# Pairs of weight blocks by seven products: the last sum of a chain by an accumulating transfer, the stream's steps spread over all 28 steps of a pair

## The chip, the cores and the metric

The kernel runs on one core of a Trainium2 chip. The metric is the device time of one execution in microseconds (us). Five engines work beside each other, each through its own instruction list in order: PE (TensorE: matrix products, with its weight loads shown as PEld), DVE (VectorE), ACT (ScalarE), POOL (GpSimd) and SP (SyncE, which here only issues DMA transfers). The transfers run on 16 DMA engines that all queues share. Products go to PSUM, everything else lies in SBUF.

## The reference

Two layers over 256 tokens of width 2048, in float32, then a last norm:

```python
x = x + even_layer(x, ...)     # norm, one wide projection, a gated linear recurrence, dilated attention, projection back
x = x + odd_layer(x, ...)      # the layer in which the change lies
return rms_norm(x, final_norm)

def odd_layer(x, norm, w_in, ...):
    h = rms_norm(x, norm)
    z = h @ w_in               # 2048 -> 512, 512, 1024, 16, 1024, 1024, 1024, 1024
    q, k, v, a_lr, gc, u, vd, gd = jnp.split(z, ...)
    ...                        # chunked linear attention from q, k, v; spatial gating from u, vd; gates gc, gd
    return jnp.concatenate([yc, yd], axis=-1) @ w_out
```

The change touches only how `h @ w_in` is computed for q with k, for the two halves of vd, and for the two halves of u.

## The kernel before, in words

**A weight tile.** Weights come from HBM in tiles of 128 x 1024 float32 (512 KB: two of the 16 k-tiles, 512 columns each). Products run in a rounded format, so every tile is split first (`parts`, L135): ACT casts it to `whi` (L138), DVE subtracts to get `wlo` (its line shows as L73, that of the helper). There are four `whi` and four `wlo` tiles, so a tile can be cast as soon as PE is done with the fourth tile before it. Each product is three matmuls of 512 columns (high by high, high by low, low by high).

**Two kinds of work.** A plain block (`token_steps`) multiplies each weight tile with both token blocks: 12 matmuls a tile (L146 to L148). A *pair* takes two column blocks of 512 at once, splits tokens and rows of the weights into halves, and needs seven products of half size instead of eight (a scheme of the Strassen kind): 7 x 4 = 28 steps of one tile and 6 matmuls each (L251 to L253). There are three pairs, one after the other: q with k (units 6 and 10 of `w_in1`), vd (14, 18) and u (30, 34). Four plain blocks, the gates, are the *stream* between the pairs' steps: 32 stream steps, of which the pairs take 10, 8 and 10, and the last four come after the third pair.

**The steps of a pair** (numbered 0 to 27 here, four to a product):

- 0 to 3: product into `m12` from the tiles `x0` (block a, upper rows); after a step has split its tile, POOL issues an accumulating transfer (L245) that adds block b's upper rows to the tile in place. Before each step SP is handed the fetch of a tile of `y0` (block b, lower rows).
- 4 to 7: `m3` from `y0`; then block b's upper rows are added to `y0` in the same way.
- 8 to 11: `m56` from the new `x0`; then block b's lower rows are added to `x0`.
- 12 to 15: `m7` from the new `y0`.
- 16 to 19: `m56` again, from the new `x0`.
- 20 to 23: `m12` again, from fresh tiles `z0` (block a, lower rows), fetched by SP.
- 24 to 27: `m4` from `x0` with block a's lower rows added.

In the kernel before the last of these sums is one DVE instruction a tile, `x0 + z0` (L299), and the steps of the last two products alternate: `z0[0]`, `z0[1]`, `z0[2]`, `m4` 0, `z0[3]`, `m4` 1, 2, 3. The adds are held in program order among them. When the seven products are there, DVE joins them (L279 to L283, L301). During the steps of `z0` the first tiles of the next pair are fetched too (`onward`, into the buffers that `y0` has left).

**Buffers and queues.** Tiles rest in three rings: `raw` with three buffers (stream tiles and `z0`), `rx` and `ry` with four each (`x0` and `y0`, whose roles swap from pair to pair). All fetches go through SP's one queue, whose instructions wait in order for their buffer to come free. The accumulating transfers go through POOL's queue.

**The order.** `weave` (L217) decides where stream steps stand: after each step of the pair it lets the stream go on while `done * 17 < taken * count`, so all stream steps of a pair stand among its first 17 steps (for a count of 10: after steps 0, 1, 3, 5, 6, 8, 10, 11, 13 and 15). Small tasks (the linear attention, the gates, transposes) are interleaved by `tick`, which counts steps.

Of the kernel before, what the change touches and what calls it, by code (L numbers as in the profile page):

```python
# [13 lines left out]
ALU = mybir.AluOpType  # L14
# [37 lines left out]
def trunk(ctx, tc, x, xt, lead, w_in0, w_out0, w_va, w_in1, w_out1, w_gate, small, dist, cst, w_alpha, w_s,  # L52
          r_balpha, r_vnorm, r_fnorm, out):
    nc = tc.nc
# [29 lines left out]
    def mid_tile(shape, name, dtype=F32):  # L84
        return mid.tile(shape, dtype, name=name, tag="mid")
# [13 lines left out]
    def tick(n):  # L99
        for task in list(tasks):  # L100
            task[1] -= n
            if task[1] <= 0:
                wait = next(task[0], None)
                if wait is None:
                    tasks.remove(task)
                else:
                    task[1] = wait
# [11 lines left out]
    def raw_tile(shape, tag=None):  # L119
        if tag is None:  # L120
            tag = "raw"
            if not paired[0]:
                turns.append(turns.pop(0))
                tag = turns[-1]
        return rawp.tile(shape, F32, name=tag, tag=tag, bufs=rings[tag])
# [9 lines left out]
    def parts(raw, n=1024):  # L135
        hi = hip.tile([P, n], F32R, name="whi", tag="whi")
        lo = lop.tile([P, n], F32R, name="wlo", tag="wlo")
        nc.scalar.copy(hi, raw)  # L138
        sub(lo, raw, hi)
        return hi, lo  # L140
# [68 lines left out]
    def piece_of(w, u, i):  # L209
        return w[u + i // 2][:, i % 2 * 1024:i % 2 * 1024 + 1024]  # L210

    def fetch(w, u, i, tag):
        raw = raw_tile([P, 1024], tag)
        nc.sync.dma_start(out=raw, in_=piece_of(w, u, i))
        return raw

    def weave(steps, stream, count):  # L217

        done = taken = 0
        while True:  # L220
            try:
                next(steps)
            except StopIteration as end:
                return end.value
            taken += 1
            while done < count and done * 17 < taken * count:
                stream.step()
                done += 1

    def pair(w, ua, ub, act, forms, x0, tag, after=None):  # L230

        f3, f5, f6, f7 = forms

        def step(ps, a, i, raw, first, u=None):
            tile_, k0, b = a
            hi, lo = parts(raw)
            if u is not None:
                nc.gpsimd.dma_start(out=raw, in_=piece_of(w, u, i), accum_op=ALU.add)  # L245
            for kk in range(2):
                j = 2 * i + kk
                wh, wl = hi[:, kk * 512:(kk + 1) * 512], lo[:, kk * 512:(kk + 1) * 512]
                xh = tile_[:, k0 + j, b * P:(b + 1) * P]
                xl = tile_[:, k0 + j, T + b * P:T + (b + 1) * P]  # L250
                nc.tensor.matmul(ps, xh, wh, start=(first and j == 0), stop=False, skip_group_check=not first)  # L251
                nc.tensor.matmul(ps, xh, wl, start=False, stop=False, skip_group_check=not first)  # L252
                nc.tensor.matmul(ps, xl, wh, start=False, stop=(j == 7), skip_group_check=not first)  # L253
                tick(1)

        def run(ps, a, raws, first, u=None):
            for i, raw in enumerate(raws):
                step(ps, a, i, raw, first, u)
                yield

        def bank():
            return psm.tile([P, 512], F32, name="ps", tag="ps")

        m12, m3, m56, m7 = bank(), bank(), bank(), bank()
        y0 = []
        for i, raw in enumerate(x0):
            y0.append(fetch(w, ub + 2, i, tag))
            step(m12, (act, 0, 0), i, raw, True, ub)
            yield
        s1 = mid_tile([P, 512], "s1")  # L270
        nc.scalar.copy(s1, m12)
        yield from run(m3, f3, y0, True, ub)
        yield from run(m56, f5, x0, True, ub + 2)
        s5 = mid_tile([P, 512], "s5")
        nc.scalar.copy(s5, m56)
        yield from run(m7, f7, y0, True)
        yield from run(m56, f6, x0, False)
        t = mid_tile([P, 512], "t")
        nc.vector.tensor_tensor(out=t, in0=m56, in1=s1, op=ALU.subtract)  # L279
        c22 = s1  # L280
        nc.vector.tensor_tensor(out=c22, in0=m7, in1=t, op=ALU.add)
        nc.vector.tensor_tensor(out=t, in0=m3, in1=t, op=ALU.add)
        nc.vector.tensor_tensor(out=s5, in0=s5, in1=c22, op=ALU.subtract)  # L283
        m4 = bank()
        onward = []
        z0 = []
        for i in range(6):
            if i < 4:
                z0.append(fetch(w, ua + 2, i, "raw"))
                step(m12, (act, 8, 0), i, z0[i], False)  # L290
                yield
                if after is not None:
                    onward.append(fetch(w, after, i, tag))
            if i > 1:
                step(m4, (act, 8, 1), i - 2, x0[i - 2], True)
                yield
            if 0 < i < 5:

                tc.keep_in_program_order(nc.vector.tensor_tensor(out=x0[i - 1], in0=z0[i - 1], in1=x0[i - 1],  # L299
                                                                 op=ALU.add))  # L300
        nc.vector.tensor_tensor(out=s5, in0=m4, in1=s5, op=ALU.add)  # L301
        return [m12, s5], [t, c22], onward

# [499 lines left out]
    paired[0] = True  # L803
    x0 = [fetch(w_in1, 6, i, "rx") for i in range(4)]
    ps, ps_k, x0 = weave(pair(w_in1, 6, 10, act2, forms2, x0, "ry", 14), stream, 10)
    drain()
    eb, enb, ebl = decays
# [81 lines left out]
    vf = []  # L889
    mv = tiny.tile([P, 8, 2], F32, name="mv", tag="mv", bufs=1)  # L890
    *vd, x0 = weave(pair(w_in1, 14, 18, act2, forms2, x0, "rx", 30), stream, 8)
    for c, ps in enumerate(vd):
        t = big_tile([P, 2, 512], f"vf{c}")
# [53 lines left out]
    def mix(c, t):  # L947
        yield 2
        for b in range(2):
# [7 lines left out]
            yield 2  # L957

    *ud, _ = weave(pair(w_in1, 30, 34, act2, forms2, x0, "ry"), stream, 10)
    paired[0] = False  # L960
    for c, ps in enumerate(ud):
# [52 lines left out]
    for s in range(4):  # L1014
        raw = raw_tile([P, 4, 256])
# [118 lines left out]
```

## Time and profile before

| | |
|---|---|
| median of 3 runs | 883.27 us (882.65 to 884.69) |
| the profiled execution | 882.66 us, its span 881.0 us |
| PE, PEld | 857.9 us busy (97%), 718.6 us (82%) |
| DVE, ACT, POOL | 610.0 us (69%), 526.3 us (60%), 42.9 us (5%) |
| SP's DMA queue q1 | 152.65 MB, 50.8% of the 16 engines' span |
| POOL's DMA queue q0 | 22.06 MB, 12.6% |

The span runs from the first instruction to the last. Busy time is that of instructions which compute. Matmuls overlap, so the duration of one (389 ns for 512 columns) is longer than the distance from one to the next. A "DMA share" is the time that packets took, over the 16 engines and the stretch. The three pairs run from about 537 us to 767 us.

### The profile page before, as it was taken

To read this page: it belongs to the slowest core of one execution; us is meant where nothing else is said; L and a number is where in the kernel's file an instruction comes from. 1 tells how busy PE (TensorE), PEld (TensorE's weight loads), DVE (VectorE), ACT (ScalarE), POOL (GpSimd) and SP (SyncE) were. 2 spreads that over 40 slices of the span, in tenths; PEclk is the share of its full clock that TensorE was granted. 3 is DMA by queue.
4 is the path that set the end of the run, shared out by engine and by line. 5 is a ranking of instruction groups with operands and counts; after the bars stand their busy time and mean duration, and the time that the engine had idled before them with its cause. 6 is when DMAs were issued, how large, how long until landed. Compare 5 with 4: busy or idle time off the path is not lost.

```text
span 881.0 us, 11887 instructions
## 1 busy us (share of the span) xinstructions
PE 857.9 (97%) x4408; PEld 718.6 (82%) x4408; DVE 610.0 (69%) x867; ACT 526.3 (60%) x764; POOL 42.9 (5%) x60
## 2 busy tenths in 40 slices
PE   8999999999999999999999999998999899899996
PEld 7888888888888888888888988885768578688886
DVE  7676557677576586666555996679748976995652
ACT  7755556666766766554444776565476766654532
POOL 1100000000000000010000002201210121000000
PEclk9999999999999999999999999999999999999999
DMA  9896555555455455565544658967965899665502
GB/s 342 335 366 213 185 194 164 170 169 177 160 177 170 144 172 178 190 208 194 184 135 154 219 184 209 252 225 211 250 144 176 245 254 322 202 220 189 190 2 96
DMA packets 50266, 175.53 MB, mean 199 GB/s; under 512 B 5648, under 2 KB 6160, under 8 KB 49952
## 3 DMA queue, kind: packets, MB, share of 16 engines
q1 hardware_dynamic: 43920, 152.65, 50.8%
q0 software_dynamic: 6144, 22.06, 12.6%
q8 instruction: 34, 0.56, 0.2%
q14 instruction: 24, 0.20, 0.1%
q10 hardware_dynamic: 144, 0.07, 0.0%
HBM read 172.66 MB, written 2.10 MB: 198 GB/s over the span
## 4 chain that ended last, share of the span: by engine, by line
PE 91%; DVE 6%; ACT 1%; issue 1%; DMA 0%; ACTq 0%
PE pc L315 20%; PE ps L147 15%; PE ps L148 15%; PE ps L146 15%; PE pc L314 10%; PE ps L251 3%; PE ps L252 3%; PE ps L253 3%; DVE wlo L73 3%; ACT whi L138 1%; DVE rx L299 1%; PE pc L317 1%; PE sc L500 1%; PE gp L584 1%; PE gp L583 1%
## 5 line engine op out<-in xcount | busy, mean ns | idle before, releaser
L315 PE MATMUL pc<-act,whi 128*128 128x512 f32 x768 | 269.8, 395 | 0.0
L314 PE MATMUL pc<-act,wlo 128*128 128x256 f32 x720 | 208.5, 290 | 0.0
L73 DVE TENSOR_TENSOR wlo<-rx,whi 128x1024 fp32r<-128x1024 f32 (+2 forms) x118 | 141.4, 1199 | 74.9 <-ACT whi L138 73.3
L138 ACT CAST whi<-rx 128x1024 fp32r<-128x1024 f32 (+1 forms) x115 | 119.9, 1044 | 100.3 <-PE ps L148 59.1
L73 DVE TENSOR_TENSOR wlo<-ry,whi 128x1024 fp32r<-128x1024 f32 (+2 forms) x110 | 131.6, 1198 | 67.9 <-ACT whi L138 66.7
L315 PEld LDWEIGHTS pc<-act,whi 128*128 128x128 f32 x768 | 142.6, 188 | 29.4
L138 ACT CAST whi<-ry 128x1024 fp32r<-128x1024 f32 (+1 forms) x108 | 112.2, 1041 | 90.4 <-PE ps L148 53.2
L73 DVE TENSOR_TENSOR wlo<-raw,whi 128x1024 fp32r<-128x1024 f32 (+2 forms) x100 | 119.0, 1190 | 47.7 <-ACT whi L138 45.7
L138 ACT CAST whi<-raw 128x1024 fp32r<-128x1024 f32 (+1 forms) x97 | 100.9, 1040 | 68.0 <-PE ps L148 25.6
L314 PEld LDWEIGHTS pc<-act,wlo 128*128 128x128 f32 x720 | 135.9, 189 | 2.4 <-DVE wlo L73 0.8
L146 PE MATMUL ps<-whi,act 128*128 128x512 f32 (+2 forms) x352 | 131.8, 377 | 1.4 <-DVE la_s L473 1.1
L147 PE MATMUL ps<-wlo,act 128*128 128x512 f32 (+2 forms) x352 | 131.0, 372 | 1.3 <-DVE wlo L73 1.2
L148 PE MATMUL ps<-whi,act 128*128 128x512 f32 (+2 forms) x352 | 130.7, 371 | 0.0
L146 PE MATMUL ps<-whi,yt 128*128 128x512 f32 (+1 forms) x256 | 97.3, 380 | 0.0
L148 PE MATMUL ps<-whi,yt 128*128 128x512 f32 (+1 forms) x256 | 96.4, 376 | 0.0
L147 PE MATMUL ps<-wlo,yt 128*128 128x512 f32 (+1 forms) x256 | 96.2, 376 | 0.0
L146 PEld LDWEIGHTS ps<-whi,act 128*128 128x128 f32 x352 | 66.1, 188 | 15.0 <-issue 2.2
L147 PEld LDWEIGHTS ps<-wlo,act 128*128 128x128 f32 x352 | 66.3, 188 | 13.5 <-DVE wlo L73 2.6
L148 PEld LDWEIGHTS ps<-whi,act 128*128 128x128 f32 x352 | 66.2, 188 | 11.4
L148 PEld LDWEIGHTS ps<-whi,yt 128*128 128x128 f32 x256 | 48.2, 188 | 8.9
L147 PEld LDWEIGHTS ps<-wlo,yt 128*128 128x128 f32 x256 | 48.2, 188 | 8.5
L146 PEld LDWEIGHTS ps<-whi,yt 128*128 128x128 f32 x256 | 48.2, 188 | 8.3
(289 smaller groups left out, 1040.1 us busy)
## 6 DMA issues: line engine op xcount, KB each, us to landing
raw<-in_w_in SPq DMA_DIRECT2D x77, 512.0 KB, 5.2
ry<-in_w_in SPq DMA_DIRECT2D x64, 512.0 KB, 4.7
rx<-in_w_in SPq DMA_DIRECT2D x63, 512.0 KB, 4.6
rx<-in_w_out SPq DMA_DIRECT2D x24, 512.0 KB, 4.3
ry<-in_w_out SPq DMA_DIRECT2D x23, 512.0 KB, 4.0
rx<-in_w_in POOLq DMA_DIRECT2D x20, 512.0 KB, 9.9
raw<-in_w_out SPq DMA_DIRECT2D x17, 512.0 KB, 4.5
ry<-in_w_in POOLq DMA_DIRECT2D x16, 512.0 KB, 8.6
```

Of the source, the lines that this page charges most:

```text
L73: nc.vector.tensor_tensor(out=o, in0=a, in1=hi.bitcast(F32), op=ALU.subtract)
L138: nc.scalar.copy(hi, raw)
L146: nc.tensor.matmul(ps[b], xh, wh, start=first, stop=False)
L147: nc.tensor.matmul(ps[b], xh, wl, start=False, stop=False)
L148: nc.tensor.matmul(ps[b], xl, wh, start=False, stop=last)
L251: nc.tensor.matmul(ps, xh, wh, start=(first and j == 0), stop=False, skip_group_check=not first)
L252: nc.tensor.matmul(ps, xh, wl, start=False, stop=False, skip_group_check=not first)
L253: nc.tensor.matmul(ps, xl, wh, start=False, stop=(j == 7), skip_group_check=not first)
L299: tc.keep_in_program_order(nc.vector.tensor_tensor(out=x0[i - 1], in0=z0[i - 1], in1=x0[i - 1], op=ALU.add))
L314: nc.tensor.matmul(ps[c][:, 1, :], wl, act[:, k, 0:T], start=False, stop=False)
L315: nc.tensor.matmul(ps[c], wh, act[:, k, :], start=(k == 0), stop=(k == KT - 1))
L317: nc.tensor.matmul(ps[c][:, 1, :], wl, act[:, k, 0:T], start=False, stop=False)
```

## The change

The weave spreads a pair's stream steps over all 28 steps: `done * 28 < taken * count` (for a count of 10: after steps 0, 2, 5, 8, 11, 14, 16, 19, 22 and 25; for 8: after 0, 3, 7, 10, 14, 17, 21 and 24). The second run of `m56` now issues an accumulating transfer of block a's lower rows into `x0` after each split, four more for a pair. The DVE adds are gone, the `z0` tiles are no longer kept after their split, and the last two products run one after the other.

```diff
@@ weave
-            while done < count and done * 17 < taken * count:
+            while done * 28 < taken * count:
                 stream.step()
                 done += 1
@@ pair
-        yield from run(m56, f6, x0, False)
+        yield from run(m56, f6, x0, False, ua + 2)
@@
-        z0 = []
-        for i in range(6):
-            if i < 4:
-                z0.append(fetch(w, ua + 2, i, "raw"))
-                step(m12, (act, 8, 0), i, z0[i], False)
-                yield
-                if after is not None:
-                    onward.append(fetch(w, after, i, tag))
-            if i > 1:
-                step(m4, (act, 8, 1), i - 2, x0[i - 2], True)
-                yield
-            if 0 < i < 5:
-                tc.keep_in_program_order(nc.vector.tensor_tensor(out=x0[i - 1], in0=z0[i - 1], in1=x0[i - 1],
-                                                                 op=ALU.add))
+        for i in range(4):
+            step(m12, (act, 8, 0), i, fetch(w, ua + 2, i, "raw"), False)
+            yield
+            if after is not None:
+                onward.append(fetch(w, after, i, tag))
+        yield from run(m4, (act, 8, 1), x0, True)
```

## Rows read from the trace of the kernel before

**Rows 1.** The page's first part: busy us, share of the span, instructions.

```profile
PE 857.9 (97%) x4408; PEld 718.6 (82%) x4408; DVE 610.0 (69%) x867; ACT 526.3 (60%) x764; POOL 42.9 (5%) x60
```

**Rows 2.** Windows: for each pair steps 0 to 15, then 16 to 27.

```profile
core 0: us, PE busy (x) PEld busy (x) DVE busy (x) ACT busy (x) POOL busy (x), PEclk, DMA share, GB/s
537.40:586.40 49.00, 49.00 (x218) 40.56 (x217) 32.50 (x27) 31.29 (x33) 9.42 (x11) 1.00 1.01 265
586.40:609.30 22.90, 18.89 (x76) 13.13 (x75) 21.20 (x23) 12.01 (x13) 0.00 (x0) 1.00 0.47 151
609.30:671.50 62.20, 62.08 (x295) 45.52 (x294) 41.86 (x52) 38.12 (x57) 10.28 (x12) 1.00 0.87 216
671.50:693.80 22.30, 17.94 (x72) 12.83 (x71) 20.48 (x23) 14.57 (x16) 0.00 (x0) 1.00 0.46 156
693.80:745.60 51.80, 50.63 (x224) 41.60 (x223) 41.74 (x56) 33.52 (x36) 11.40 (x14) 1.00 1.02 269
745.60:767.00 21.40, 18.45 (x74) 13.04 (x72) 19.13 (x21) 13.54 (x15) 0.00 (x0) 1.00 0.63 217
```

**Rows 3.** Waits in 586.4 to 609.3: total us, times, longest us.

```profile
ACT whi L138 <- DVE rx L299: 6.1, 4, 3.0
...
ACT whi L138 <- DMA raw<-in_w_in: 3.0, 1, 3.0
PE ps L251 <- ACT whi L138: 2.8, 4, 1.3
```

**Rows 4.** Groups on DVE, 537 to 771: count, busy us, mean ns.

```profile
L73 DVE TENSOR_TENSOR wlo<-rx,whi 128x1024 fp32r<-128x1024 f32 x40 | 48.7, 1220 | 22.9 <-ACT whi L138 21.9
...
L299 DVE TENSOR_TENSOR rx<-raw,rx 128x1024 f32<-128x1024 f32 x8 | 9.7, 1216 | 0.0
L299 DVE TENSOR_TENSOR ry<-raw,ry 128x1024 f32<-128x1024 f32 x4 | 4.9, 1218 | 0.0
```

**Rows 5.** Timeline of PE, an undisturbed step: start us, duration us.

```profile
538.10 0.39 PE L251 MATMUL ps<-whi,act 128*128 128x512 f32 x1
538.32 0.39 PE L252 MATMUL ps<-wlo,act 128*128 128x512 f32 x1
538.55 0.39 PE L253 MATMUL ps<-whi,act 128*128 128x512 f32 x1
```

**Rows 6.** DMA in 543.9 to 581.4: packets, MB, share; issues with us to landing.

```profile
q0 software_dynamic: 1439, 5.24, 73.3%
q1 hardware_dynamic: 1178, 4.30, 30.8%
...
rx<-in_w_in POOLq DMA_DIRECT2D x5, 512.0 KB, 10.0
```

**Rows 7.** Timeline of POOL: issues of the accumulating transfers at steps 1, 11.

```profile
537.66 0.86 POOL L245 DMA_DIRECT2D rx<-in_w_in  x1 [6.12 <-DVE wlo L73]
...
570.94 0.86 POOL L245 DMA_DIRECT2D rx<-in_w_in  x1 [1.93 <-issue]
...
731.93 0.85 POOL L245 DMA_DIRECT2D rx<-in_w_in  x1 [2.62 <-issue]
```

**Rows 8.** Tile `raw` in 537 to 586, 586 to 609, 700 to 745.

```profile
DMA to landing us min/median/max: 5.2/7.9/9.3
...
DMA to landing us min/median/max: 4.0/4.5/5.4
...
DMA to landing us min/median/max: 6.6/8.2/11.7
```

**Rows 9.** Tile `raw` in 537 to 771: cast durations ns min/median/max.

```profile
L138 ACT CAST whi<-raw x40: 1037/1055/1067, 538.2 to 769.0; 128x1024 fp32r<-128x1024 f32 x40
```

**Rows 10.** Timeline of SP: first pair, fetches of `z0[2]`, `z0[3]`.

```profile
581.59 0.33 SPq L214 DMA_DIRECT2D raw<-in_w_in  x1
592.81 0.33 SPq L214 DMA_DIRECT2D raw<-in_w_in  x1
```

**Rows 11.** Timeline of ACT, third pair: cast of `z0[2]`, with its wait.

```profile
751.45 1.05 ACT L138 CAST whi<-raw 128x1024 fp32r<-128x1024 f32 x1 [1.89 <-DMA raw<-in_w_in]
```

## The prediction

> **What bounds the kernel now.** I read the page's busy times first, then windows over the three pairs, then waits, timelines and DMA queues inside them. PE is the bound: 97% of the span, the next engine 69% [rows 1]. So the change can give no more than the time in which PE stands still inside the pairs, and it can take that back by new stops. The windows cut each pair where the stream's steps end [rows 2]. In steps 0 to 15, with all the stream steps between, PE is busy without a gap in the first two pairs, and the 16 DMA engines are full: shares of 1.01, 0.87 and 1.02. In steps 16 to 27 it is the other way round: PE idles 22.9 - 18.9 = 4.0, 22.3 - 17.9 = 4.4 and 21.4 - 18.4 = 3.0 us, 11.3 us together, DVE is busy 21.2 of 22.9 us, and the DMA share falls to 0.47, 0.46 and 0.63. The granted clock is 1.00 in all six.
>
> The waits of the first such tail name the stop: PE's first matmul of a step waits for ACT's cast, and the cast waited 6.1 us for the DVE adds of L299 (four of them) and once 3.0 us for a `raw` transfer [rows 3]. That transfer is `z0[3]`: its fetch is issued at 592.81, 11 us after that of `z0[2]` at 581.59, because the three `raw` buffers are held until the first add is done [rows 10].
>
> So DVE and the ring stop the tails, and the transfers fill the first parts. The change moves work from the first kind of limit to the second.
>
> **What goes.** Twelve adds of 1.22 us (8 and 4) [rows 4] are 14.6 us of DVE. PE's matmuls follow each other every 0.227 us (538.10, 538.32, 538.55) [rows 5]: a pair step of 6 is 1.365 us, a stream step of 12 is 2.73 us. One split costs DVE 1.22 us, so a tail without stream steps asks 16 splits' worth of DVE (12 splits, 4 adds: 19.5 us, and the joining of the products besides) for 12 x 1.365 = 16.4 us of PE. After the change the same 12 pair steps have 4 stream steps among them (3 in the second pair): 16 splits, still 19.5 us, but 16.4 + 10.9 = 27.3 us of PE. DVE is then no limit there. What PE gets back is at least the 11.3 us of idle. At most it is the tails' whole excess over the matmul pace, 22.9 + 22.3 + 21.4 - 3 x 16.4 = 17.4 us, which counts the small tasks' matmuls as if they were free. I take 13.5, nearer to the idle, since those tasks stay.
>
> **What it adds on POOL and the DMA engines.** Four accumulating transfers a pair, 12 in all. POOL's part is 12 x 0.86 us [rows 7], beside an engine busy 5%: nothing, unless the ring behind it is full; POOL already waits by "issue" before step 11's, and nothing but these transfers stands behind it. On the DMA engines the window 543.9 to 581.4 gives the price [rows 6]. q0 holds 73.3% of 37.5 us for 5.24 MB, ten tiles, so 2.75 us a tile; q1 holds 30.8% for 8.2 tiles, 1.41 us a tile. An accumulated tile costs twice a plain one, and the sum for the new ones is 4 x 2.75 = 11.0 us a pair. The `z0` fetches stay. The pairs' DMA time is now 49.5 + 10.8 = 60.3, 54.1 + 10.3 = 64.4 and 52.8 + 13.5 = 66.3 us [rows 2]; it becomes 71.3, 75.4 and 77.3, against PE busy times of 67.9, 80.0 and 69.1. In the first pair and the third the transfers ask as much time as the pair has; some of it is prefetch for what follows (in the third `w_out` tiles) and can be late.
>
> The Trainium skill, DMA: Bandwidth & Descriptors (Anatomy of one DMA), prices a transfer from GpSimd at about 2.0 us fixed, mostly completion, plus bytes / 436e3. By it a 512 KB tile moves in an estimated 1.2 us whatever it does on the way, the 12 would cost 14.4 us instead of 33, and the first rival below is what would come. The rows' 2.75 us speaks against it.
>
> **Are the new sums in time?** From step 16 to step 24 lie 8 x 1.365 + 3 x 2.73 = 19.1 us. An accumulating transfer needs 0.9 to issue and 10.0 to land [rows 6, 7], the cast before the matmul 1.05 [rows 9] and about 0.25 to hand over: 12.2. They are in time with 7 us to spare, so I price them at nothing; the cover is gone if the queue is 7 us behind. The tighter ones are those of steps 8 to 11. The last is issued at 570.94, 33.5 us into the pair, and lands some 10 us later, at 43.5. Step 19 needs it 1.3 us before its start. Before, ten stream steps stand ahead of step 19, after it seven, so it starts 8.2 us sooner, at 19 x 1.365 + 7 x 2.73 = 45.0, and needs its tile at 43.7. The eight us of spare are spent. Fewer stream fetches ahead (three, 4.2 us) give some back. In the third pair the last issue is at 731.93, 38.1 us in. I take 0 and keep 2 us a pair for the range.
>
> **The fetches of `z0`: the new wait.** Steps 19 to 25 now use seven `raw` tiles (stream, `z0[0]`, `z0[1]`, `z0[2]`, stream, `z0[3]`, stream) where a ring of three holds them. `z0[2]` gets the buffer of the stream tile after step 19. That one can be cast when PE is done with the stream step after 16 (four `whi` tiles). From there: cast and subtraction 2.6, issue 0.3, landing L, cast and hand-over 1.3, so 4.2 + L. PE meanwhile works 5 pair steps and one stream step, 9.6 us. The stop is L - 5.4. The stream tile after step 25 hangs on `z0[2]` in the same way: 2.7 + L against 8.2 us, again L - 5.5. Behind the waiting fetch SP holds the `onward` fetches and the next stream tile; the next pair's tiles wait with them, needed only at its first steps.
>
> All depends on L. In the tail of the first pair, where no accumulation runs, it is 4.5 us; in the first part 7.9 (5.2 to 9.3), in the third pair 8.2 and up to 11.7 [rows 8], and there `z0[2]` already kept ACT waiting 1.9 us, at 751.45 [rows 11]. After the change the accumulations run through the tail, and four fetches for what follows stand in the same queue. I take L = 9.0 for `z0[2]` in pairs one and three (between the medians and the longest) and 6.2 for the last stream tile, when the accumulations have nearly landed: 3.6 + 0.7 = 4.3 us each. In the second pair, whose small tasks stretch it and whose DMA share is lower, I take L = 7.0: 1.6 us. Ends: L = 4.5 costs nothing; L = 11.7 and 8 cost 6.3 + 2.5 = 8.8 in two pairs and some 4 in the other, 21.6 us.
>
> **The sum.** 13.5 back, 4.3 + 1.6 + 4.3 = 10.2 us given up again: 3.3 us net. The profiled execution took 882.66 us (1.66 more than its span) and becomes 879.4; the median of the runs is 0.6 above it, so 880.0.
>
> **Rivals.**
> - *The transfers fit.* L stays near 5.4, the whole stop goes: 869 to 873, about 871.5. For it: the tails use half of the DMA engines' time, and no first part stops PE for a transfer today. Against it: the sums per pair above.
> - *The DMA engines become the bound.* Place: `z0[1]` to `z0[3]` and the stream tiles among them, behind the next pair's fetches and shared with four more accumulations. Price: L - 5.4 and L - 5.5 a pair. It decides where both L average above 7.7, for then 3 x 4.5 us eat the 13.5. At the upper ends, 21.6 - 13.5 = 8 us slower; about 887 in the middle. For it: 71.3 us of transfers in a pair that lasts 71.9. Plain fetches took 7.9 us beside accumulations and 4.5 without. The Trainium skill, same page (Queues, rings and completion order), says that each DMA engine takes the queues with work in turns, packet by packet; by it a plain tile among accumulations takes an estimated 1.41 + 2.75 = 4.2 us of its queue instead of 1.4. Seven in a row would then be 29 us. The two values of L agree with it.
> - *It does not do what it says.* Instructions are put in order by a planner; if it hoists the new transfers' users or holds the stream tiles back, the tails stop as before: 883.
>
> **How the numbers follow.** Transfers fit 0.22 (871.5); forecast 0.43 (876 to 884 about 880); DMA bound 0.27 (887); no effect 0.08 (883). A measurement here can tell 0.2%, 1.8 us, from nothing: below 881.5 is faster, above 885.0 slower. The first case and two thirds of the second are faster (0.51), the rest of the second with the last and a little of the third is no change (0.22), 0.27 slower. The range takes in the first case's middle and the dearer half of the third: 871.5 to 889; the forecast's own is 876 to 884.
>
> **What would show it.** The DVE adds gone, DVE's share in steps 16 to 27 down from above 0.9 to about 0.75, and DMA shares near 1 in both parts of pairs one and three. ACT's casts wait for "DMA raw" in a tail more than the 3.0 us of the first pair today, at `z0[2]` and later, and `raw` landings lie between 7 and 10 us. If casts of `rx` or `ry` wait for POOL's transfers for more than 2 us a pair, the step on the sums' timing was wrong. If `raw` lands within 6 us in the tails, the first rival is right.

## The result: 893.34 us, 1.1% slower

The changed kernel takes 893.34 us (median of 4 runs, 892.16 to 895.23); the kernel before took 883.6 beside it. The ratio is 1.0112 (95% interval 1.009 to 1.0133). The forecast of 880.0 and its upper end of 889 were both missed. The profiled execution after has a span of 891.3 us, 10.3 more than before.

The page's first part, of the kernel after (answers to [rows 1]):

```profile
PE 864.8 (97%) x4408; PEld 725.1 (81%) x4408; DVE 597.0 (67%) x855; ACT 525.9 (59%) x764; POOL 52.8 (6%) x72
```

The DVE adds are gone (13.0 us, 12 instructions) and POOL has twelve more issues: the change does what it says. But PE is busy 6.9 us longer with the same 4408 matmuls, and idle 891.3 - 864.8 = 26.5 us instead of 23.1. These two, 6.9 and 3.4, are the 10.3. Both need a cause: a longer wait doesn't make PE busier.

Windows of the kernel after, cut as in [rows 2] (stretch and its length; busy us of PE, PEld, DVE, ACT, POOL; granted clock; DMA share; GB/s):

```profile
538.00:576.10 38.10, 38.10 (x170) 31.55 (x169) 26.44 (x23) 24.56 (x26) 10.29 (x12) 1.00 1.01 234
576.10:614.50 38.40, 31.70 (x122) 24.08 (x121) 23.86 (x26) 19.06 (x20) 2.93 (x4) 0.87 0.85 257
614.50:668.70 54.20, 54.20 (x262) 39.22 (x261) 35.65 (x43) 32.43 (x52) 11.68 (x14) 1.00 0.89 214
668.70:697.10 28.40, 25.26 (x109) 19.95 (x108) 22.02 (x27) 20.45 (x22) 1.85 (x3) 1.00 0.91 251
697.10:736.80 39.70, 39.61 (x174) 32.01 (x173) 34.52 (x50) 26.92 (x30) 10.34 (x13) 1.00 1.03 244
736.80:778.00 41.20, 34.46 (x121) 25.99 (x120) 22.23 (x22) 20.64 (x23) 4.41 (x6) 0.83 0.95 290
```

The first parts are shorter, as three or four stream steps have left them, and full as before. In the tails of the first and third pair PE idles 6.7 us each, more than before, though DVE is now busy for only 0.62 and 0.54 of the stretch. And the clock, 1.00 everywhere before, is 0.87 and 0.83 there. From the first matmul of a pair to the first of the next (to the end of the last one in the third pair), the pairs last 76.5, 82.6 and 81.0 us, against 72.3, 84.5 and 74.7: 8.7 us more.

What PE waited for in the first tail, 576.1 to 614.5 (answers to [rows 3]: total us, times, longest):

```profile
ACT whi L138 <- DMA raw<-in_w_in: 12.7, 4, 6.5
...
PE ps L250 <- ACT whi L138: 5.5, 4, 2.9
```

ACT's 6.1 us behind DVE's adds have gone, 12.7 us behind `raw` transfers stand in their place, and PE's matmuls wait up to 2.9 us for the casts, where 1.3 was the longest. SP's fetches before and in that tail show why (answers to [rows 10]; start, duration of the group):

```profile
563.42 0.33 SPq L132 DMA_DIRECT2D raw<-in_w_in  x1
564.79 3.53 SPq L214 DMA_DIRECT2D ry<-in_w_in  x3
570.22 0.33 SPq L214 DMA_DIRECT2D raw<-in_w_in  x1
571.59 0.33 SPq L214 DMA_DIRECT2D ry<-in_w_in  x1
574.31 8.49 SPq L214 DMA_DIRECT2D raw<-in_w_in  x2
```

The `raw` issues of L214 at 570.22 and 574.31 are `z0[0]` and `z0[1]` (the second of the last group is `z0[2]`). The four `ry` are tiles of the next pair. In the code each is asked for after a step of `z0`; the planner, which puts the instructions in order, issued them when `m7` had left their buffers: three ahead of `z0[0]` and the fourth ahead of `z0[1]`, though both are used earlier. In the kernel before, all four went ahead of `z0[2]`, but `z0[0]` went ahead of them and only two ahead of `z0[1]`, and the cast of `z0[0]` came so late that it waited for PE alone:

```profile
569.87 0.33 SPq L214 DMA_DIRECT2D raw<-in_w_in  x1
571.23 3.05 SPq L214 DMA_DIRECT2D ry<-in_w_in  x2
575.32 0.33 SPq L214 DMA_DIRECT2D raw<-in_w_in  x1
579.32 1.47 SPq L214 DMA_DIRECT2D ry<-in_w_in  x2
...
587.93 1.05 ACT L138 CAST whi<-raw 128x1024 fp32r<-128x1024 f32 x1 [0.31 <-PE ps L253]
```

After the change `z0[0]` is issued at about the same time, and ACT is ready for it at 581.2 already, as fewer stream steps stand ahead of it. The casts of `z0[0]` and `z0[1]` on ACT, with their waits:

```profile
587.66 1.04 ACT L138 CAST whi<-raw 128x1024 fp32r<-128x1024 f32 x1 [6.48 <-DMA raw<-in_w_in]
594.32 1.04 ACT L138 CAST whi<-raw 128x1024 fp32r<-128x1024 f32 x1 [5.61 <-DMA raw<-in_w_in]
```

From issue to cast that is 17.4 and 20.0 us. The DMA views of 538 to 592.8 (packets, MB, share; then the median from issue to landing) and, last, of the tile `raw` for fetches issued in 538 to 576:

```profile
q0 software_dynamic: 2147, 7.86, 73.3%
q1 hardware_dynamic: 1589, 5.78, 28.9%
...
ry<-in_w_in SPq DMA_DIRECT2D x4, 512.0 KB, 14.8
...
DMA to landing us min/median/max: 5.3/8.5/19.9
```

q0 takes 0.733 x 54.8 us for 15 tiles, 2.68 us each; q1 0.289 x 54.8 for 11, 1.44 each, so both prices of [rows 6] hold. The seven fetches that begin between 563.42 and 574.31 need until 594.2 (574.31 + 19.9), 4.4 us a tile: their own 1.4 and about one accumulated tile between. The rule of turns in the Trainium skill, DMA: Bandwidth & Descriptors (Queues, rings and completion order), gave an estimated 4.2 for a tile, and the 4.4 of this trace agree with it.

The clock is the other half. Windows of 2 us around these two stops:

```profile
586.00:588.00 2.00, 0.89 (x4) 0.39 (x3) 0.00 (x0) 0.34 (x1) 0.00 (x0) 1.00 1.03 264
588.00:590.00 2.00, 0.50 (x1) 0.19 (x1) 1.23 (x1) 0.71 (x1) 0.00 (x0) 0.88 1.05 279
590.00:592.00 2.00, 1.98 (x5) 1.50 (x5) 0.00 (x0) 0.00 (x0) 0.00 (x0) 0.50 1.08 274
592.00:594.00 2.00, 0.52 (x2) 0.00 (x0) 0.00 (x0) 0.00 (x0) 0.00 (x0) 0.50 1.00 348
594.00:596.00 2.00, 0.58 (x1) 0.29 (x1) 0.60 (x1) 1.47 (x2) 0.00 (x0) 0.50 0.52 213
596.00:598.00 2.00, 1.53 (x4) 1.13 (x4) 1.96 (x3) 1.97 (x3) 0.00 (x0) 0.50 0.13 35
598.00:600.00 2.00, 2.00 (x6) 1.53 (x6) 1.93 (x4) 2.00 (x3) 0.00 (x0) 0.56 0.84 266
```

PE works 1.39 us in the first 4, then the granted clock stands at 0.50, the 1.2 GHz level, until about 599.8. PE's matmuls in that time:

```profile
588.76 0.50 PE L250 MATMUL ps<-whi,act 128*128 128x512 f32 x1 [1.87 <-ACT whi L138]
590.02 0.80 PE L251 MATMUL ps<-wlo,act 128*128 128x512 f32 x1 [0.76 <-DVE wlo L73]
...
591.04 0.63 PE L250 MATMUL ps<-whi,act 128*128 128x512 f32 x1
591.46 0.63 PE L251 MATMUL ps<-wlo,act 128*128 128x512 f32 x1
591.89 0.63 PE L252 MATMUL ps<-whi,act 128*128 128x512 f32 x1
595.41 0.79 PE L250 MATMUL ps<-whi,act 128*128 128x512 f32 x1 [2.89 <-ACT whi L138]
```

They follow each other every 0.425 us instead of 0.227 [rows 5]. In [rows 3] PE's longest wait for a cast was 1.3 us, and the clock stayed at 1.00. Slow matmuls in the first and the third tail make the 6.9 us of extra busy time, though not all of it is lost: in part of it PE would have waited for the next tile.

In the third pair the clock fell first behind another wait, that for a sum of steps 8 to 11 in `rx`. The cast is that of step 19, and the windows follow it:

```profile
744.06 1.04 ACT L138 CAST whi<-rx 128x1024 fp32r<-128x1024 f32 x1 [2.46 <-DMA rx<-in_w_in]
746.00:748.00 2.00, 1.59 (x4) 1.31 (x5) 1.49 (x2) 0.05 (x1) 0.00 (x0) 0.63 1.06 268
748.00:750.00 2.00, 2.00 (x6) 1.54 (x6) 0.77 (x1) 1.05 (x1) 1.41 (x2) 0.52 1.05 281
```

The cast of `z0[1]` then waits 6.57 us and PE 3.35, and the clock falls again.

### The profile page after: what moved, and what is told of

It is laid out like the page before. It is cut to its first block, busy times and chain, and to the rows that moved or that the text cites. A ratio compares the mean times of both kernels' runs of the same rounds, so it can differ in the third digit from the quotient of the medians.

```text
span 891.3 us, 11905 instructions
## 1 busy us (share of the span) xinstructions
PE 864.8 (97%) x4408; PEld 725.1 (81%) x4408; DVE 597.0 (67%) x855; ACT 525.9 (59%) x764; POOL 52.8 (6%) x72
## 4 chain that ended last, share of the span: by engine, by line
PE 89%; DMA 6%; DVE 2%; ACT 1%; issue 1%; ACTq 0%; DVEq 0%
PE pc L305 20%; PE ps L147 14%; PE ps L148 14%; PE ps L146 13%; PE pc L304 10%; DMA raw<-in_w_in 6%; PE ps L251 3%; PE ps L250 3%; PE ps L252 3%; DVE wlo L73 1%; ACT whi L138 1%; PE pc L307 1%; PE sc L490 1%; PE gp L574 1%; PE gp L573 1%
## 5 line engine op out<-in xcount | busy, mean ns | idle before, releaser
L73 DVE TENSOR_TENSOR wlo<-rx,whi 128x1024 fp32r<-128x1024 f32 (+2 forms) x118 | 141.0, 1199 | 76.9 <-ACT whi L138 76.1
L138 ACT CAST whi<-rx 128x1024 fp32r<-128x1024 f32 (+1 forms) x115 | 119.7, 1044 | 86.5 <-PE ps L148 42.5
L148 PEld LDWEIGHTS ps<-whi,yt 128*128 128x128 f32 x256 | 48.2, 188 | 8.9
L147 PEld LDWEIGHTS ps<-wlo,yt 128*128 128x128 f32 x256 | 48.2, 188 | 8.4
L146 PEld LDWEIGHTS ps<-whi,yt 128*128 128x128 f32 x256 | 48.2, 188 | 8.3
```

The source lines that it names most:

```text
L73: nc.vector.tensor_tensor(out=o, in0=a, in1=hi.bitcast(F32), op=ALU.subtract)
L146: nc.tensor.matmul(ps[b], xh, wh, start=first, stop=False)
L147: nc.tensor.matmul(ps[b], xh, wl, start=False, stop=False)
L148: nc.tensor.matmul(ps[b], xl, wh, start=False, stop=last)
```

## The experiments

Three theories stand against each other. By *order*, the `z0` tiles come late because of the order in SP's queue and the turn of three `raw` buffers. By *load*, the sum of the DMA work is too large, wherever it stands. By *sums*, the new accumulations land late. In the expectations, theory A is the load of the added accumulations (in `late_next` with two readings, the queue as the place or the sum as the limit) and D the sum of the DMA work; B and C are order (B: the spread's stream tiles take the ring's buffers; C: too few buffers turn too slowly). All kernels do the same 4408 matmuls, but for the operand in `no_last_sum`. A span is the start of the first pair (537.4 to 539.3 us), the pairs, and what lies behind them.

| kernel | median us | ratio (95%) | three pairs, us | behind them | PE busy, idle |
|---|---|---|---|---|---|
| before | 883.6 | 1 | 72.3 84.5 74.7 = 231.5 | 112.0 | 857.9, 23.1 |
| after | 893.34 | 1.0112 (1.009 to 1.0133) | 76.5 82.6 81.0 = 240.2 | 113.4 | 864.8, 26.5 |
| spread_only | 897.38 | 1.0154 (1.0136 to 1.0172) | 74.1 90.2 82.4 = 246.6 | 111.7 | 866.8, 28.9 |
| accum_only | 886.67 | 1.0023 (1.001 to 1.0036) | 72.0 86.5 74.4 = 232.9 | 113.6 | 862.6, 22.8 |
| no_last_sum | 873.32 | 0.9881 (0.9866 to 0.9896) | 67.4 80.1 73.5 = 221.0 | 114.1 | 856.4, 16.1 |
| late_next | 886.23 | 1.0019 (1.0006 to 1.0032) | 72.3 89.5 73.7 = 235.5 | 113.7 | 866.7, 21.7 |
| raw4_lo3 | 891.48 | 1.0085 (1.0066 to 1.0104) | 76.1 83.0 79.6 = 238.7 | 113.8 | 865.9, 25.9 |
| late_next_raw4 | 881.07 | 0.9973 (0.9959 to 0.9987) | 72.5 83.8 73.5 = 229.8 | 113.8 | 860.1, 21.1 |
| z_first | 875.86 | 0.9902 (0.9886 to 0.9919) | 67.5 79.2 70.0 = 216.8 | 120.0 | 857.0, 17.3 |
| dve_z_first | 875.36 | 0.9904 (0.988 to 0.9928) | 68.1 83.8 72.0 = 223.9 | 112.0 | 856.9, 16.3 |

Each ratio is to the kernel before as timed beside that run. Pairs and busy times are of the profiled execution, whose span is 1.7 us less than its time; a pair counts 168 matmuls of its own three lines, and sums are rounded last.

**Each part alone.** `spread_only` has the kernel before with the even spread; `accum_only` has the changed kernel with the old rule.

```diff
# spread_only, against the kernel before
-            while done < count and done * 17 < taken * count:
+            while done * 28 < taken * count:
# accum_only, against the kernel after
-            while done * 28 < taken * count:
+            while done < count and done * 17 < taken * count:
```

> The kernel before with the even spread alone: the last sum stays on DVE, no transfer is added. Theory A (the four added accumulations a pair fill the DMA engines, so that the z0 tiles come late and PE stands still and loses its clock): the loss goes, 873 to 881 us, ACT's casts wait for raw transfers less than 12 us in the pairs, granted clock 1.00 in all tails. Theory B (the spread itself does the damage: stream tiles between the z0 tiles take the ring of three raw buffers): still slow, 887 us or more, with the long waits for raw at steps 20 to 23 as in the changed kernel.

> The changed kernel with the stream's steps among a pair's first 17 as before: the accumulating transfer alone. Theory A: 33 us more of transfers, but they fall into tails whose DMA share was 0.47 to 0.63, while steps 16 to 24 are only 10.9 us apart and a sum needs 12 us to be there, so PE stops for the sums (casts of rx and ry wait for transfers) for 1 to 4 us a pair: 880 to 890 us. Theory B: without stream tiles in the tails the ring is free, the DVE adds are gone: 870 to 876 us.

The spread alone is the slowest of these, 13.8 us over before, where a gain was held possible. Its `z0` tiles stay in the ring of three until their add, with stream tiles now asking for the same three. ACT's waits in its three pairs, 537 to 780:

```profile
ACT whi L138 <- DMA raw<-in_w_in: 31.4, 13, 7.0
```

The kernel after has the same total, 31.7 us. `accum_only` loses only 3 us. Its one wait for `raw` in the first tail is 6.3 us, and its casts wait for a summed tile once in all pairs, 0.3 us: the theory of the sums has nothing to stand on there. So neither part gains in itself, and to be rid of DVE's adds was not what the even spread needed first: the last kernels below show that it needed `z0` elsewhere.

**Without the last sum.** This kernel leaves out the accumulation of block a's lower rows, so its last product `m4` multiplies the old tiles.

```diff
-        yield from run(m56, f6, x0, False, ua + 2)
+        yield from run(m56, f6, x0, False)
```

> The changed kernel without the last sum: the accumulations after steps 16 to 19 are left out, so m4 is formed from x0 without block a's lower rows (that part of the computation is missing). Spread, order and z0 fetches as in the changed kernel. Theory A: 33 us less of DMA time, the late z0 tiles are in time, 868 to 876 us, raw landings in the tails below 8 us. Theory B: the ring still stops the tails, 886 us or more.

20 us come back by taking away 33 us of DMA work. Order and load both explain that: without the accumulations the queue in front of `z0` moves on. It says what these transfers cost as they are arranged here, not what a better arrangement can give.

**The order in SP's queue.** The next pair's tiles are asked for at the step of `z0[3]` and held there; after the third pair the next eight fetches are held behind it too. (The last argument, new in `fetch`, keeps the instruction in program order; that edit and the one for the eight fetches aren't shown.)

```diff
         for i in range(4):
             step(m12, (act, 8, 0), i, fetch(w, ua + 2, i, "raw"), False)
+            if i == 3 and after is not None:
+                for j in range(4):
+                    onward.append(fetch(w, after, j, tag, True))
             yield
-            if after is not None:
-                onward.append(fetch(w, after, i, tag))
```

> The changed kernel with the fetches for what follows a pair (the next pair's first tiles, after the third pair the next eight tiles) held in SP's queue behind the fetch of z0[3]; same transfers, same bytes, only their order. Theory A with the queue as the place: the z0 tiles no longer stand behind three or four tiles at 3.9 us each, 876 to 884 us, longest raw landing below 10 us instead of 13.0. Theory A with the sum of DMA work as the limit: the order matters little, 889 to 894 us. Theory B: 889 to 894 us.

7.1 us better with the same bytes, which load does not explain, but 2 us short of the range expected. SP's fetches around its first tail, then the cast of `z0[2]`:

```profile
571.60 12.57 SPq L218 DMA_DIRECT2D raw<-in_w_in  x3
...
586.56 0.33 SPq L218 DMA_DIRECT2D raw<-in_w_in  x1
586.94 1.91 SPq L218 DMA_DIRECT2D ry<-in_w_in  x4
```

```profile
592.21 1.04 ACT L142 CAST whi<-raw 128x1024 fp32r<-128x1024 f32 x1 [6.93 <-DMA raw<-in_w_in]
```

`z0[0]` and `z0[1]` are now in time, and the four `ry` go out only behind `z0[3]` (586.56). The stop has moved to `z0[2]`, whose fetch (the last of the three, at 583.84) waited for its buffer and takes 8.4 us to its cast. That is the stop of the prediction, at its place and near its L of 9: PE stands still for 2.32 and 0.76 us, where L - 5.4 gives 3.0. The tails still slow the clock: PE is busy 866.7 us, so all of the loss against before in this execution is slow matmuls, and its idle time is less. The execution is the slowest of its ten, 890.11 us. In it the first and the third pair are 4.2 and 7.3 us shorter than in the kernel after, but the second is 6.9 us longer: a `raw` tile's cast at 679.59 waits 5.00 us, and PE's clock falls there too. So holding the next tiles back isn't a gain in every pair.

**A fourth `raw` buffer**, paid for with one `wlo` buffer, alone and with the order mended.

```diff
-    lop = pool("lop", 4)
+    lop = pool("lop", 3)
@@
-    rings = {"raw": 3, "rx": 4, "ry": 4}
+    rings = {"raw": 4, "rx": 4, "ry": 4}
```

> The changed kernel with four raw buffers instead of three, paid for with one of the four wlo tiles. Theory C: the stop goes from L - 5.4 to about L - 8 for the same tiles: the waits for raw in the tails fall from 27 us to below 10, 876 to 884 us; a loss of 1 to 2 us by the missing wlo tile is inside that. Theory D: 889 us or more.

> The run with the next fetches held behind z0[3] (886.2 us) with a fourth raw buffer, paid for with one of the four wlo tiles. There the first stop stood at the fourth tile of the row: z0[2] fetched only when the ring had room, and landed 8 us later. If that turn of three buffers is what is left after the queue's order: 876 to 881 us, the longest wait of a cast for raw in the first tail from 6.9 to below 3 us. If it is the work of the DMA engines: 884 us or more.

Alone it gives 1.9 us, far less than expected, and its interval overlaps that of the kernel after. `z0[0]` is now fetched first, but three next tiles still stand ahead of `z0[1]` and the fourth ahead of `z0[2]`, whose casts wait 4.01 and 6.60 us:

```profile
565.09 0.33 SPq L214 DMA_DIRECT2D raw<-in_w_in  x1
566.45 4.41 SPq L214 DMA_DIRECT2D ry<-in_w_in  x3
571.89 0.33 SPq L214 DMA_DIRECT2D raw<-in_w_in  x1
573.25 0.33 SPq L214 DMA_DIRECT2D ry<-in_w_in  x1
577.33 0.33 SPq L214 DMA_DIRECT2D raw<-in_w_in  x1
```

With the next tiles behind `z0` the same buffer gives 5.2 us, and the longest wait for `raw` in the first tail falls from 6.9 to 3.5. So both causes are real, and the queue's order hides most of the buffer's. What three `wlo` tiles cost by themselves wasn't measured.

**`z0` in its own buffers.** `y0` is done with after step 15, so its four buffers can hold `z0`. A first try changed the ring's name (in the two kernels with DVE adds it also asks for a next tile only after the add that frees its buffer):

```diff
-            step(m12, (act, 8, 0), i, fetch(w, ua + 2, i, "raw"), False)
+            step(m12, (act, 8, 0), i, fetch(w, ua + 2, i, tag), False)
```

> The changed kernel with the z0 tiles fetched into the four buffers that y0 has left, and the next pair's x0 into them after that; the three raw buffers hold stream tiles alone. Same transfers, same bytes. Theory C (the place of the loss is the ring: seven tiles of steps 19 to 25 go through three buffers, each busy for a landing of 8 us and more): z0 can be fetched at steps 12 to 15, no cast of z0 waits, the granted clock stays at 1.00, 870 to 878 us. Theory D (the sum of DMA work is the limit, wherever the tiles lie): 885 to 893 us, and the casts wait at other tiles (x0, the stream).

> The same buffers, with the accumulating transfer, but the stream's steps among the first 17 as in the kernel before. Theory C: the stop at z0[3] (6.3 us of waiting in the first pair with the raw ring) goes, what is left is the sum that has 10.9 us from step 16 to 24: 876 to 883 us, slower than with the even spread by 3 us or more. Theory D: about as with the raw ring, 884 to 888 us.

> The even spread with the last sum on DVE as before, z0 in y0's buffers, next x0 fetched after each add. 33 us less of DMA time than with the accumulations, 14.6 us of DVE more, in tails that now have 27 us of PE work. Theory C: the 897 us of the spread with DVE adds came from the three raw buffers that each add held longer; without that 868 to 876 us, as good as the accumulation or better. Theory B (the spread itself is the harm): 888 us or more.

> The kernel before with one edit: z0 in y0's buffers (stream among the first 17 steps, last sum on DVE). It tells what share of the 11 to 17 us of PE's stops in the old tails came from the ring (z0[3] fetched only after the first add) and what from DVE. Theory C with DVE as the tails' limit: the wait for z0[3] (3.0, 2.8 and 4.2 us of ACT) goes, DVE stays the limit, 878 to 883 us. If the ring was most of it: below 875 us.

(`early` has the old rule of 17, `dve` the DVE adds.) These were 890.41, 897.43, 887.44 and 894.11 us, ratios 1.0066 (1.0044 to 1.0087), 1.014 (1.0112 to 1.0168), 1.0029 (1.0015 to 1.0043) and 1.0105 (1.0078 to 1.0132). The edit didn't test what was meant. Buffers of a ring go round in the order of the text, `z0[0]`, next tile, `z0[1]`, next tile, so the next pair's tiles took two of the four, and `z0[2]` waited for `z0[0]`'s. With the DVE adds one next tile still stands ahead of `z0[3]`, whose cast waits 9.06 us in `dve_z_in_y`. In `z_in_y` the cast of `z0[2]` waits:

```profile
596.52 1.04 ACT L138 CAST whi<-ry 128x1024 fp32r<-128x1024 f32 x1 [9.42 <-DMA ry<-in_w_in]
```

The second try asks for all four first:

```diff
         onward = []
+        z0 = [fetch(w, ua + 2, i, tag) for i in range(4)]
         for i in range(4):
-            step(m12, (act, 8, 0), i, fetch(w, ua + 2, i, "raw"), False)
+            step(m12, (act, 8, 0), i, z0[i], False)
```

> As the run with z0 in y0's buffers, mended: there the fetches were written in the order z0[0], next[0], z0[1], next[1], so the next pair's tiles took two of the four buffers and z0[2] waited for z0[0] to be split. Here all four z0 fetches stand first, each tile of what follows takes a buffer only when z0 has left it. Theory C (the loss is the turn of too few buffers at steps 19 to 25, at landings of 8 us and more): no cast of z0 waits over 1 us, 870 to 878 us. Theory D (the sum of DMA work): 885 us or more, with the waits moved to x0 or the stream.

> Even spread, last sum on DVE, no added transfer, all four z0 fetches first into y0's buffers, a next tile only after the add that frees its buffer. Theory C: 868 to 877 us, since it has neither the ring nor the 33 us of transfers. If the next pair's x0, fetched only after the adds, comes too late for its first steps (they lie 5 to 8 steps on), the casts wait for ry at the start of the second pair: 880 to 888 us. Theory D: about as fast as the kernel without the last sum, 873 us.

`dve_z_first` is the kernel before with the spread of 28, `z0` fetched in the same way, and each next tile asked for after the add. Both beat both kernels, 875.86 and 875.36 us. Windows over the first pair of `z_first`, and its fetches of `z0`:

```profile
538.00:575.50 37.50, 37.50 (x168) 31.03 (x167) 25.85 (x23) 24.14 (x25) 9.94 (x12) 1.00 1.02 236
575.50:605.00 29.50, 27.82 (x122) 22.48 (x121) 23.70 (x25) 18.92 (x19) 2.72 (x4) 1.00 1.04 333
```

```profile
564.43 3.53 SPq L214 DMA_DIRECT2D ry<-in_w_in  x3
...
571.23 0.33 SPq L214 DMA_DIRECT2D ry<-in_w_in  x1
```

The tail takes 29.5 us instead of 38.4, at DMA shares of 1.02 and 1.04, higher than in the kernel after, and the clock is 1.00. As the reason for the tails' stops, load falls: all accumulations are there, the engines are full, and PE stands still 1.7 us. Against `no_last_sum`, which moves 33 us less, it is 2.5 us slower. Landing is no faster than in the kernel after (up to 19.9 us for `ry` in this stretch); the tiles are only asked for early enough, and of the `z0` casts that of `z0[3]` alone waits, 2.73 us, against the 1 us expected. A stop of the same kind then comes behind the third pair, at a stream tile issued at 744.15 behind `w_out` tiles:

```profile
744.15 0.33 SPq L132 DMA_DIRECT2D rx<-in_w_in  x1
```

```profile
756.68 1.05 ACT L138 CAST whi<-rx 128x1024 fp32r<-128x1024 f32 x1 [4.41 <-DMA rx<-in_w_in]
```

PE then stops for 3.33 us, the clock is 0.51 in 760 to 765, and the part behind the pairs takes 120.0 us instead of 112.0: of 14.7 us gained in the pairs, 8.0 are given back. Whether order or load is the cause there isn't shown: the engines are full until 760, and `dve_z_first`, with 33 us less of transfers, takes 112.0.

**The spread's worth when `z0` is in time.** The same two kernels with the old rule of 17.

> The accumulating transfer with all four z0 fetches first into y0's buffers, but the stream's steps among the first 17: it lacks only the even spread against the run at 875.9 us. Steps 16 and 24 are 10.9 us apart, a sum needs about 12 us, the transfers have the half idle tails: the casts of x0's tiles wait 1 to 4 us a pair, 877 to 884 us. If the spread adds nothing: 874 to 877 us.

> The kernel before with all four z0 fetches first into y0's buffers and nothing else: stream among the first 17 steps, last sum on DVE. It lacks only the even spread against the run at 875.4 us. If DVE is the limit of a tail without stream steps (16 splits' worth of 1.22 us and the joining for 16.4 us of PE): 878 to 883 us, casts in the tails wait for the DVE adds as before, only the wait for z0[3] gone. If the ring alone made the old tails slow: 874 to 877 us.

881.88 us, ratio 0.9972 (0.9954 to 0.9989), and 883.53, ratio 1.0001 (0.999 to 1.0011). The even spread is thus worth 6.0 and 8.2 us, and with the DVE adds `z0` in its own buffers gives nothing without it: DVE stays the limit of the old tails, as the prediction had it, and ACT's casts wait 21.6 us for the adds in the pairs, 11.8 in the kernel before. The accumulating transfer instead of the DVE add is worth 1.7 with the old rule and nothing measurable with the new one. By the prediction's own terms a tail with four stream steps asks DVE for 19.5 us, with the adds 24.4, and PE for 27.3, so the adds should have room. Not all have it: in the pairs of `dve_z_first` ACT's casts wait 19.9 us for them, and the pairs are 7.1 us longer than in `z_first`. The totals are the same because `z_first` gives 8.0 back behind the pairs.

## Why the prediction was wrong

**Right: what goes.** 13.5 us were to come back; in `z_first` the pairs are 14.7 us shorter than before. Both parts of the change bring them, once `z0` is in time: in the pairs the even spread gives 8.1 us (232.0 in `dve_z_first_early`, 223.9 in `dve_z_first`) and the leaving of DVE, with the last two products in a row, 7.1 (216.8 in `z_first`). The prediction let prefetch for what follows be late at no price; in `z_first` the part behind the pairs is 8.0 us longer, and so a kernel without the late `z0` gains 7.7 us in all.

**Right: the size of the transfers.** Shares times lengths of the windows after give 38.5 + 32.6 = 71.1, 48.2 + 25.8 = 74.0 and 40.9 + 39.1 = 80.0 us of DMA time in the pairs, against 71.3, 75.4 and 77.3. The price of an accumulated tile held (2.68 against 2.75). The estimate from the Trainium skill, DMA: Bandwidth & Descriptors (Anatomy of one DMA), was 1.2 us a tile; for accumulated tiles the 2.68 contradict it.

**Off in the third pair: the sums.** They were priced at 0 with up to 2 us a pair. Casts of `rx` waited 6.3 us in all, three times, 4.8 of them in the third pair: by the prediction's own sign the timing of the sums of steps 8 to 11 was wrong there. With the old rule (`accum_only`) it was 0.3. What they cost by themselves no run separates, since PE then waits for `z0[1]` in any case.

**Wrong: L, and the tile it stands at.** The failed step is "I take L = 9.0 for `z0[2]` in pairs one and three". It put the waits of `z0[0]` and `z0[1]` at nothing and let the `onward` fetches wait *behind* `z0[2]`. The first was so in the first tail before; the second was not even there, where all four went ahead of `z0[2]` and cost nothing because the `z0` tiles were needed late. With the stream steps moved, three next tiles went ahead of `z0[0]` and the fourth ahead of `z0[1]`, both were needed some 7 us sooner, and from issue to cast they took 17.4 and 20.0 us. `late_next` holds the next tiles back, and 8.4 us stand at `z0[2]`. The price given up, 4.3 + 1.6 + 4.3 = 10.2 us, was in fact 9.0, 3.4 and 11.0 against the pairs of `z_first`: 23.4 us, over twice as much.

**Not seen: the clock.** Every term was priced at 0.227 us a matmul. A stop behind a transfer costs its length and then slow matmuls: against `z_first` the kernel after has, over the whole span, 7.8 us more busy time for the same matmuls and 9.2 us more idle. How much of the 7.8 PE would have waited anyway, no run separates.

The rival of the DMA engines as the bound had the place (behind the next pair's fetches) and the sign. Its reason was half right: the sharing makes each fetch slow, but in `z_first` other buffers and another order carry the same bytes through the first tail with 1.7 us of stops.

## What to carry to other kernels

When transfers fill the engines, price a new fetch by its place in its queue, not by its size: count the tiles that can be issued ahead of it, times the time of one beside the other queue (here 7 x 4.4 us). Give what is needed next its own buffers and ask for it first; here a prefetch whose buffer came free earlier went ahead, though the code asked for it later. And when a change moves work in time, read anew the order of the queue and when each tile is needed: the trace before promises neither.

## What the hardware showed that was not expected

PE's granted clock fell to the 1.2 GHz level after stops of 1.87 and 0.76 us with one matmul between, and stayed there for about 10 us, through another of 2.89, with matmuls every 0.425 us. In the third pair it fell behind PE's stops of 0.80 and 0.75 us with one matmul between, and stood at 0.50 again behind a stop of 3.35 us, where ACT had waited 6.57 us for `z0[1]`. Beside a queue of accumulating transfers a plain 512 KB tile, in a row of seven, took 4.4 us, though its own packets take 1.4: about one accumulated tile (2.7) came between. PE's busy time for the same 4408 matmuls ranges from 856.4 to 866.8 us in these kernels, so "busy 97%" hid up to 10 us of loss.
